# Two levels of an HGRN2 intra-chunk product as small matmuls at column positions of the TensorE array

## The chip, the core and the metric

The kernel runs on one core of a Trainium2 chip (trn2). A core has a matrix engine (TensorE, PE in the profile, with its weight loads shown apart as PEld), a vector engine (DVE), a scalar engine (ACT), GpSimd (POOL), a queue for transfers (SP) and 16 DMA engines. Matrix products are written to PSUM, and everything else lives in SBUF, both with 128 partitions. A matmul here has two operands: the stationary one, which a weight load (LDWEIGHTS) puts into the array, and the moving one, which streams through it.

The metric is the device time of one execution in microseconds (us). Before the change it is **1333.13 us**, the median of three runs (1332.87, 1333.13 and 1337.91).

## The reference

One layer of a decoder trunk on 512 tokens of width 1024: a wide projection feeds an mLSTM branch and an HGRN2 branch, the two are gated and merged, then a normalisation, a SwiGLU feed-forward block and a second normalisation. The change touches the HGRN2 branch alone, whose recurrence the reference writes in chunks:

```python
def step(state, xs):
    qc, kc, vc, lfc = xs
    a = jnp.cumsum(lfc, axis=2)
    rel = jnp.where(causal, a[:, :, :, None, :] - a[:, :, None, :, :], -jnp.inf)
    scores = jnp.einsum('bhtk,bhtsk,bhsk->bhts', qc, jnp.exp(rel), kc)
    o = (jnp.einsum('bhts,bhsv->bhtv', scores, vc)
         + jnp.einsum('bhtk,bhkv->bhtv', qc * jnp.exp(a), state))
    ...
```

For each of 8 heads (key size 128, value size 128), token t receives from every earlier token s the value of s, weighted by a product over the 128 key channels in which the forget gates between s and t enter channel by channel.

## The kernel before, in words

Everything is in 32-bit floats. The large projections split each operand into a high and a low part (`split`, lines 88 and 89: ACT writes the high part, DVE the low one) and add three products of the parts (`mm3`, lines 84 to 86). Each projection of 128 columns is 24 such matmuls with 512 moving columns, or, in `natural_proj`, many with 256 moving columns. Weights arrive through `load_w` and are split into three rotating buffers each, `whi` and `wlo` (lines 98 and 99).

The HGRN2 branch works on pairs of heads, `pr` = 0 to 3. `h_units` computes the forget gate f, the key K, the query Q, the value v and the output gate of a pair by projections. Then `h_chain` cuts the weights between tokens into levels. At a level with half-size `hs`, the tokens are cut into blocks of 2·hs, and the product of the K of each first half with the Q of the second half gives the weights across the middle of that block. After each level `h_advance` (lines 592 and 593) multiplies Q of the second halves and K of the first halves by the gates of their neighbours, so that the next level can use them; both are DVE operations of 128x512. The levels are hs = 1, 2 (by vector products), then 4, 8, 16, 32, 64, 128 and 256 by `h_level`.

In `h_level`, the levels 4, 8, 16 and 32 share one form: for each of the two heads (c) and each of the four tiles of 128 tokens (j), one matmul at line 646 has all 128 tokens of K as its stationary operand and the 64 tokens of Q that lie in second halves as its moving one. Its result is 128x64 in the PSUM tile `lps`, and for hs = 16 and 32 only hs·hs blocks of it are copied out, by ACT at line 673, to `ad`, the matrix of weights inside a tile. The level 64 (line 651) multiplies 64 stationary by 64 moving tokens, and 128 and 256 (lines 657 and 663) larger ones. A 32-bit matmul that is not split is two weight loads and two multiplies in the trace, called passes below, so the eight matmuls of a level are 16 passes.

The steps of a pair's chain are not run at once. `defer(t, ...)` puts each off by t units of work, and `tick`, called between projections, releases them. So the levels of one pair run between the projections of the next pair (for the last pair, between the merge gates), and the tile framework's scheduler, which orders each engine's instructions by its own estimate of when their operands are there, settles the exact place. Engines wait for each other by semaphores; PE takes its instructions in that order.

Of the kernel before, what the change touches and what calls it, by code (L numbers as in the profile page):

```python
# [15 lines left out]
P = 128  # L16
T = 512
NT = T // P
# [18 lines left out]
def tile_hybrid_trunk(  # L37
# [22 lines left out]
    nc = tc.nc  # L60
    xd, od, win = x[0], out[0], w_in[0]

    def pool(stack, name, bufs=1, space=None, side=None):
        kw = {}
        if space is not None:
            kw["space"] = space
        if side is not None:
            kw["side"] = side
        return stack.enter_context(tc.tile_pool(name=name, bufs=bufs, **kw))
# [39 lines left out]
    def psum(pl, tag, shape=(P, 512), bufs=None):  # L109
        kw = {} if bufs is None else {"bufs": bufs}  # L110
        return pl.tile(list(shape), F32, tag=tag, name=tag, **kw)
# [60 lines left out]
    px = pool(st_m, "px", bufs=2, space=PSUM)  # L172
# [334 lines left out]
    px = pool(st_px, "px2", bufs=5, space=PSUM)  # L507
# [80 lines left out]
    def h_advance(st, hs):  # L588
        nb = T // hs
        qv, kv = h_halves(st, hs)  # L590
        tv = st["cur"].rearrange("p (b two) -> p b two", two=2)
        nc.vector.tensor_mul(qv[:, :, 1, :], qv[:, :, 1, :], tv[:, :, 0:1].to_broadcast([P, nb, hs]))
        nc.vector.tensor_mul(kv[:, :, 0, :], kv[:, :, 0, :], tv[:, :, 1:2].to_broadcast([P, nb, hs]))
        if hs < 128:
            nt_ = st["tot"][:, st["toff"]:st["toff"] + nb]
            nc.vector.tensor_mul(nt_, tv[:, :, 0], tv[:, :, 1])
            st["cur"] = nt_
            st["toff"] += nb

    def h_place(st, ps, gs_, w, key):  # L600

        dst = st["ad"].rearrange("p j (g k) -> p j g k", k=gs_)[:, :, :, gs_ - w:]
        msk = masks[key].bitcast(U32)[:, None].to_broadcast([P, 8, P // gs_, w])
        nc.vector.copy_predicated(dst, msk, ps.rearrange("p j (g k) -> p j g k", k=w))
# [32 lines left out]
    def h_level(st, hs):  # L637

        K, Q, ad = st["K"], st["Q"], st["ad"]
        if hs < 64:  # L640
            lps = psum(px, "px", (P, 8, 64))
            for c in range(2):
                for j in range(NT):
                    js = slice(j * P, (j + 1) * P)
                    mov = Q[:, c, js].rearrange("p (g two h) -> p g two h", two=2, h=hs)[:, :, 1]
                    nc.tensor.matmul(lps[:, 4 * c + j], K[:, c, js], mov, start=True, stop=True)  # L646
        elif hs == 64:
            lps = psum(px, "px", (P, 8, 64))
            for c in range(2):
                for j in range(NT):  # L650
                    nc.tensor.matmul(lps[0:64, 4 * c + j], K[:, c, j * P:j * P + 64], Q[:, c, j * P + 64:(j + 1) * P],
                                     start=True, stop=True)
        elif hs == 128:
            lps = psum(px, "px", (P, 2, 2, P))
            for c in range(2):
                for b in range(2):
                    nc.tensor.matmul(lps[:, c, b], K[:, c, 2 * b * P:(2 * b + 1) * P],
                                     Q[:, c, (2 * b + 1) * P:(2 * b + 2) * P], start=True, stop=True)
        else:
            for c in range(2):  # L660
                lps = psum(px, "px", (P, 2, 256))
                for b in range(2):
                    nc.tensor.matmul(lps[:, b], K[:, c, b * P:(b + 1) * P], Q[:, c, 256:512],  # L663
                                     start=True, stop=True)
                nc.scalar.copy(st["a2"][:, c], lps)
            return
        h_advance(st, hs)
        if hs < 16:
            h_place(st, lps, 2 * hs, hs, hs)
        elif hs < 64:  # L670
            for g in range(64 // hs):
                rows_ = slice(2 * hs * g, 2 * hs * g + hs)
                nc.scalar.copy(ad[rows_, :, 2 * hs * g + hs:2 * hs * (g + 1)], lps[rows_, :, hs * g:hs * (g + 1)])
        elif hs == 64:
            nc.scalar.copy(ad[0:64, :, 64:128], lps[0:64])
        else:
            nc.scalar.copy(st["a1"], lps)
# [33 lines left out]
    def h_chain(st):  # L711

        steps = [(0, h_direct_0), (1, h_direct_1), (2, h_direct_2), (3, h_direct_3)]
        steps += [(t, lambda st, hs=hs: h_level(st, hs)) for t, hs in
                  ((3.5, 4), (4, 8), (4.5, 16), (5, 32), (5.5, 64), (6, 128), (6.5, 256))]
        steps += [(7 + 0.5 * c, lambda st, c=c: h_out(st, c)) for c in range(2)]
        for t, step in steps:
            if t:
                defer(t, lambda step=step: step(st))
            else:  # L720
                step(st)
# [194 lines left out]
```

## Time and profile before

| what | value |
|---|---|
| median of three runs | 1333.13 us |
| the profiled execution | 1334.2 us |
| its span, first to last instruction | 1332.5 us |
| TensorE clock granted, mean | 0.997 |
| DMA | 141.31 MB, mean 106 GB/s |

The page of the profile gives busy times per engine, then a row of digits over 40 slices of the span, then a chain of work traced back from the last instruction, then groups of instructions. In a row of a group, `128*64` is the shape of the stationary operand (partitions by columns), and `128x64` that of the moving one; `x256 | 30.5, 272` are the count, the busy time in us and the mean duration in ns of one. Durations of matmuls overlap, since the array is pipelined: the time that a run of them takes is read from the starts. A row of the timeline begins with the start and the duration in us; consecutive instructions of one kind are merged into one row with their count.

### The profile page before, as it was taken

What the parts mean: (1) busy time and instruction counts of PE and PEld (TensorE: products, weight loads), DVE (VectorE), ACT (ScalarE), POOL (GpSimd) and SP (SyncE); (2) the same over time, 40 slices, a digit from 0 to 9 for tenths busy, and PEclk for the clock granted to TensorE, in tenths of its full rate; (3) what the DMA queues carried; (4) which work ended last, traced back from release to release, by engine and by line L of the source; (5) the groups of instructions that cost most, each with busy time, mean ns of one, the idle gap of its engine ahead of it and who ended that gap; (6) DMA issues with size and microseconds to landing.
All of it is one profiled execution on the core that took longest, in us unless ns stands there. A gap on an engine that the chain in (4) does not pass through costs nothing.

```text
span 1332.5 us, 17405 instructions
## 1 busy us (share of the span) xinstructions
PE 1315.9 (99%) x7023; PEld 1136.1 (85%) x7023; DVE 753.9 (57%) x1140; ACT 537.0 (40%) x811; POOL 41.2 (3%) x78
## 2 busy tenths in 40 slices
PE   8999999999999999999999999999999999999997
PEld 7788889888988998889898988887898888888885
DVE  5764656566555755557586754345765433334575
ACT  4773553444342533332424333323773222233332
POOL 0000000000000002000000000000000000000001
PEclk9999999999999999999999999999999999999999
DMA  8222333233323323332232222235664343335672
GB/s 235 80 72 79 88 88 92 75 81 94 88 79 89 86 79 84 98 96 70 63 83 64 71 72 64 79 95 201 197 186 128 95 129 101 102 95 162 192 229 81
DMA packets 189424, 141.31 MB, mean 106 GB/s; under 512 B 5728, under 2 KB 178592, under 8 KB 189344
## 3 DMA queue, kind: packets, MB, share of 16 engines
q1 hardware_dynamic: 188288, 140.17, 37.0%
q8 instruction: 55, 0.90, 0.3%
q14 instruction: 25, 0.20, 0.0%
q10 hardware_dynamic: 1056, 0.03, 0.0%
HBM read 138.09 MB, written 2.10 MB: 105 GB/s over the span
## 4 chain that ended last, share of the span: by engine, by line
PE 97%; DVE 1%; ACT 1%; DMA 1%; issue 0%; POOL 0%; SPq 0%; DVEq 0%; POOLq 0%
PE pp L84 19%; PE pp L85 19%; PE pp L86 19%; PE pf L84 10%; PE pf L85 10%; PE pf L86 10%; PE px L646 2%; PE px L692 1%; PE s L85 1%; PE s L86 1%; PE s L84 1%; PE px L579 1%; DMA xn<-in_x_dram 1%; PE px L424 1%; PE px L663 1%; PE px L84 0%
## 5 line engine op out<-in xcount | busy, mean ns | idle before, releaser
L89 ACT CAST whi<-wraw 128x1024 fp32r<-128x1024 f32 x246 | 258.1, 1050 | 592.3 <-PE pp L85 253.8
L89 DVE TENSOR_TENSOR wlo<-wraw,whi 128x1024 fp32r<-128x1024 f32 x246 | 300.6, 1223 | 272.4 <-ACT whi L89 270.0
L84 PE MATMUL pp<-xh,whi 128*128 128x512 f32 x704 | 278.1, 395 | 0.0
L86 PE MATMUL pp<-xh,wlo 128*128 128x512 f32 x704 | 275.5, 391 | 0.0
L85 PE MATMUL pp<-xl,whi 128*128 128x512 f32 x704 | 275.4, 391 | 0.0
L86 PEld LDWEIGHTS pp<-xh,wlo 128*128 128x128 f32 x704 | 132.6, 188 | 28.3 <-issue 0.4
L84 PEld LDWEIGHTS pp<-xh,whi 128*128 128x128 f32 x704 | 132.7, 188 | 27.6 <-issue 1.0
L85 PEld LDWEIGHTS pp<-xl,whi 128*128 128x128 f32 x704 | 132.6, 188 | 26.2
L86 PE MATMUL pf<-x1h,wlo 128*128 128x512 f32 (+1 forms) x416 | 148.4, 357 | 0.8 <-DVE wlo L89 0.8
L84 PE MATMUL pf<-x1h,whi 128*128 128x512 f32 (+1 forms) x416 | 148.4, 357 | 0.0
L85 PE MATMUL pf<-x1l,whi 128*128 128x512 f32 (+1 forms) x416 | 148.3, 356 | 0.0
L84 PE MATMUL pp<-whi,xh 128*128 128x256 f32 x352 | 100.6, 286 | 0.0
L85 PE MATMUL pp<-wlo,xh 128*128 128x256 f32 x352 | 99.8, 284 | 0.0
L86 PE MATMUL pp<-whi,xl 128*128 128x256 f32 x352 | 99.5, 283 | 0.0
L86 PEld LDWEIGHTS pf<-x1h,wlo 128*128 128x128 f32 x416 | 78.6, 189 | 12.1 <-DVE wlo L89 1.0
L84 PEld LDWEIGHTS pf<-x1h,whi 128*128 128x128 f32 x416 | 78.6, 189 | 11.3
L85 PEld LDWEIGHTS pf<-x1l,whi 128*128 128x128 f32 x416 | 78.6, 189 | 11.3
L357 DVE SCALAR_TENSOR_TENSOR y<-u,cols,y 128x512 f32<-128x512 f32 x96 | 71.9, 750 | 6.1 <-ACT y L355 2.6
L85 PE MATMUL pf<-wlo,g 128*128 128x512 f32 x176 | 68.6, 390 | 0.0
L86 PE MATMUL pf<-whi,g 128*128 128x512 f32 x176 | 68.5, 389 | 0.0
L84 PE MATMUL pf<-whi,g 128*128 128x512 f32 x176 | 68.4, 389 | 0.0
L85 PEld LDWEIGHTS pp<-wlo,xh 128*128 128x128 f32 x352 | 67.5, 192 | 0.1
(251 smaller groups left out, 1940.3 us busy)
## 6 DMA issues: line engine op xcount, KB each, us to landing
wraw<-in_w_in_dram SPq DMA_DIRECT2D x110, 512.0 KB, 3.9
wraw<-in_w_ffn_down_dram SPq DMA_DIRECT2D x44, 512.0 KB, 3.6
wraw<-in_w_ffn_gate_dram SPq DMA_DIRECT2D x26, 512.0 KB, 3.9
wraw<-in_w_ffn_up_dram SPq DMA_DIRECT2D x26, 512.0 KB, 3.9
wraw<-in_w_proj_a_dram SPq DMA_DIRECT2D x16, 512.0 KB, 3.5
wraw<-in_w_out_dram SPq DMA_DIRECT2D x16, 512.0 KB, 3.8
wraw<-in_w_proj_b_dram SPq DMA_DIRECT2D x8, 512.0 KB, 4.3
xn<-in_x_dram SPq DMA_DIRECT2D x4, 512.0 KB, 5.0
```

The source lines that it names most:

```text
L84: nc.tensor.matmul(ps, lh, rh, start=start, stop=False, **kw)
L85: nc.tensor.matmul(ps, lh, rl, start=False, stop=False, **kw)
L86: nc.tensor.matmul(ps, ll, rh, start=False, stop=stop, **kw)
L89: return nc.scalar.copy(hi, src), nc.vector.tensor_sub(lo, src, hi.bitcast(F32))
L357: nc.vector.scalar_tensor_tensor(y, u[:, tap:tap + T], cwcol(tap, ch), y, op0=OP.mult, op1=OP.add)
L424: nc.tensor.transpose(tps[:, i * P:(i + 1) * P], hn[:, i, c * P:(c + 1) * P], ident)
L579: nc.tensor.matmul(ps.rearrange("p j n -> p (j n)"), ones_r, part.rearrange("p a b -> p (a b)"), start=(i == 0), stop=(i == 1))
L646: nc.tensor.matmul(lps[:, 4 * c + j], K[:, c, js], mov, start=True, stop=True)
L663: nc.tensor.matmul(lps[:, b], K[:, c, b * P:(b + 1) * P], Q[:, c, 256:512], start=True, stop=True)
L692: nc.tensor.matmul(ops[:, i], at, vc(j), start=(e == 0), stop=(e == len(terms) - 1))
```

## The change

`h_level` gets a branch of its own for hs = 16 and 32. In place of one matmul for a tile of 128 tokens there is one for each block: the K of its first half (hs tokens) is the stationary operand, the Q of its second half (hs tokens) the moving one. `tile_position=(0, s0)` puts the stationary operand at the columns s0 of the array, so that the result lands on the partitions s0 to s0 + hs of `lps`, where line 673 reads it. For hs = 16 the columns are 0, 32, 64 and 96; for hs = 32 they are 0 and 64. In the built program these matmuls are marked with an array tile of 128x32, those at line 651 with one of 128x64, and all projections with 128x128. Levels 4 and 8 keep the old form, now at line 656. The parts of `lps` that are no longer written were never read.

```diff
-        if hs < 64:
+        if hs in (16, 32):
+
+            lps = psum(px, "px", (P, 8, 64))
+            for c in range(2):
+                for j in range(NT):
+                    for g in range(64 // hs):
+                        s0 = 2 * hs * g
+                        nc.tensor.matmul(lps[s0:s0 + hs, 4 * c + j, hs * g:hs * (g + 1)],
+                                         K[:, c, j * P + s0:j * P + s0 + hs], Q[:, c, j * P + s0 + hs:j * P + s0 + 2 * hs],
+                                         start=True, stop=True, tile_position=(0, s0))
+        elif hs < 64:
             lps = psum(px, "px", (P, 8, 64))
```

For hs = 16 that is 8·4 = 32 matmuls in place of 8, and for hs = 32 it is 8·2 = 16, for each of four pairs. All lines below move down by ten.

The scheduler also moves a few neighbours. On PE, around the level hs = 32 of the first pair, the order before is (`px<-Q,K` is the level's product into PSUM; `pp<-...` are matmuls of a value projection):

```order
L86 MATMUL pp<-whi,xl 128x256
L84 MATMUL pp<-whi,xh 128x256
L646 MATMUL px<-Q,K 128x64 x8
L85 MATMUL pp<-wlo,xh 128x256
L86 MATMUL pp<-whi,xl 128x256
```

and after the change:

```order
L84 MATMUL pp<-whi,xh 128x256
L85 MATMUL pp<-wlo,xh 128x256
L647 MATMUL px<-Q,K 32x32 x16
L86 MATMUL pp<-whi,xl 128x256
L84 MATMUL pp<-whi,xh 128x256
```

The level stands one projection matmul later: 14 of them lie between the levels 16 and 32 where 13 did. This is so in the first three pairs; in the fourth, whose neighbours are 128x512 matmuls, 7 lie between them where 12 did.

On DVE, at the same place, one piece of the difference (`e<-K,Q` is the first product of the next pair, `v<-pp,vb` the value with its bias, `Q<-Q,tot` and `K<-K,tot` the advance after a level):

```order
 L89 TENSOR_TENSOR wlo<-wraw,whi 128x1024
-L571 TENSOR_TENSOR e<-K,Q 128x512
 L592 TENSOR_TENSOR Q<-Q,tot 128x16x32
 L593 TENSOR_TENSOR K<-K,tot 128x16x32
 L556 TENSOR_TENSOR v<-pp,vb 128x512
+L571 TENSOR_TENSOR e<-K,Q 128x512
 L592 TENSOR_TENSOR Q<-Q,f 128x512
 L593 TENSOR_TENSOR K<-K,f 128x512
-L571 TENSOR_TENSOR e<-K,Q 128x512
 L556 TENSOR_TENSOR v<-pp,vb 128x512
+L571 TENSOR_TENSOR e<-K,Q 128x512
```

The two products of the next pair moved behind the advance of level 32 and the values.

On DVE in the fourth pair (`wlo<-wraw,whi` is the low part of a projection's weights, `acc<-acc,sga` a merge gate that is applied; line 730 became 740):

```order
 L604 COPY_PREDICATED ad_4702<-mask_4696,px 128x64x8
-L89 TENSOR_TENSOR wlo<-wraw,whi 128x1024
 L592 TENSOR_TENSOR Q<-Q,tot 128x32x16
 L593 TENSOR_TENSOR K<-K,tot 128x32x16
-L730 TENSOR_TENSOR acc<-acc,sga 128x512
+L740 TENSOR_TENSOR acc<-acc,sga 128x512
+L89 TENSOR_TENSOR wlo<-wraw,whi 128x1024
 L592 TENSOR_TENSOR Q<-Q,tot 128x16x32
 L593 TENSOR_TENSOR K<-K,tot 128x16x32
```

The split of a weight's low part moved behind the advance of level 16 and the gate. The rows of ACT, POOL and SP stand in the same order as before.

## The prediction

> **What bounds the kernel now.** I read the page first, for the busy shares and the chain that ended last.
>
> ```profile
> PE 1315.9 (99%) x7023; PEld 1136.1 (85%) x7023; DVE 753.9 (57%) x1140; ACT 537.0 (40%) x811; POOL 41.2 (3%) x78
> ...
> PE 97%; DVE 1%; ACT 1%; DMA 1%; issue 0%; POOL 0%; SPq 0%; DVEq 0%; POOLq 0%
> ```
>
> TensorE is busy for 99% of the span and makes up 97% of the chain. The levels of the HGRN2 chain lie between 600 and 830 us. The table by windows gives busy times in the order PE, PEld, DVE, ACT, POOL, then the clock:
>
> ```profile
> 600.00:830.00 230.00, 230.00 (x1419) 204.20 (x1418) 151.27 (x221) 81.49 (x173) 6.30 (x7) 1.00 0.27 70
> ```
>
> PE has no idle time there, at full clock. DVE is busy for two thirds of it and ACT for a third, so neither sets the pace. What the change gives or costs is therefore what it does to PE's own time in this stretch. Busy PE is not PE at its peak, so I read the time of a level from starts in the timeline. Level 16 of the first pair, between projection matmuls of 256 columns:
>
> ```profile
> 617.95 0.28 PE L86 MATMUL pp<-whi,xl 128*128 128x256 f32 x1
> 617.95 1.88 PEld L646 LDWEIGHTS px<-Q,K 128*128 128x128 f32 x16
> 618.07 1.90 PE L646 MATMUL px<-Q,K 128*128 128x64 f32 x16
> ...
> 619.78 0.36 PE L84 MATMUL pp<-whi,xh 128*128 128x256 f32 x1
> ...
> 619.98 0.28 PE L85 MATMUL pp<-wlo,xh 128*128 128x256 f32 x1
> ```
>
> From the start of L86 to that of L85 are 2.03 us. L86 and L84 take 0.12 us each of these (617.95 to 618.07 is one such step), so the level costs **1.79 us**. Its 16 weight loads follow each other every (1.88 - 0.19)/15 = 0.113 us, and 16 times that is 1.8: the level is nothing but its loads of 128 columns, and its 64 moving columns are hidden behind them. The first load starts together with the projection's last multiply, so there is no gap on entry.
>
> Level 32 of the same pair, with the advance of level 16 ahead of it on DVE:
>
> ```profile
> 620.01 0.69 DVE L592 TENSOR_TENSOR Q<-Q,tot 128x512 f32<-128x512 f32 x1 [0.67 <-PE px L646]
> ...
> 620.62 0.69 DVE L593 TENSOR_TENSOR K<-K,tot 128x512 f32<-128x512 f32 x1
> ...
> 621.28 0.28 PE L84 MATMUL pp<-whi,xh 128*128 128x256 f32 x1
> 621.42 1.86 PEld L646 LDWEIGHTS px<-Q,K 128*128 128x128 f32 x16
> 621.45 1.97 PE L646 MATMUL px<-Q,K 128*128 128x64 f32 x16
> ...
> 623.23 0.36 PE L85 MATMUL pp<-wlo,xh 128*128 128x256 f32 x1
> ...
> 623.43 0.28 PE L86 MATMUL pp<-whi,xl 128*128 128x256 f32 x1
> ```
>
> Counted in the same way it is 623.43 - 621.28 - 0.24 = **1.91 us**, 0.12 more: K's advance ends at 621.31, and the first load starts behind it at 621.42, not with the multiply at 621.28. In the fourth pair the neighbours have 512 columns:
>
> ```profile
> 811.16 0.39 PE L84 MATMUL pp<-xh,whi 128*128 128x512 f32 x1
> ...
> 811.38 0.39 PE L85 MATMUL pp<-xl,whi 128*128 128x512 f32 x1
> ...
> 811.61 1.89 PE L646 MATMUL px<-Q,K 128*128 128x64 f32 x16
> ...
> 813.63 0.39 PE L84 MATMUL pp<-xh,whi 128*128 128x512 f32 x1
> ...
> 813.86 0.40 PE L85 MATMUL pp<-xl,whi 128*128 128x512 f32 x1
> ```
>
> Here 813.63 - 811.38 = 2.25, less two steps of 0.23, is 1.79: no wait. Before, the two levels take 4 x 1.79 (level 16) + 3 x 1.91 + 1.79 (level 32) = **14.68 us** of PE. No more than that, 1.1% of the time, is at stake.
>
> **The change, part by part.** It removes these 14.68 us and adds, per pair, 64 passes for level 16 and 32 for level 32, each a load and a multiply, in array tiles of 128x32. The nearest row that stands in a narrower array tile is level 64 (128x64):
>
> ```profile
> 627.26 0.28 PE L85 MATMUL pp<-wlo,xh 128*128 128x256 f32 x1
> ...
> 627.38 0.28 PE L86 MATMUL pp<-whi,xl 128*128 128x256 f32 x1
> 627.59 1.01 PEld L651 LDWEIGHTS px<-Q,K 128*64 128x64 f32 x16
> 627.59 1.15 PE L651 MATMUL px<-Q,K 128*64 128x64 f32 x16
> ...
> 628.67 0.50 PE L84 MATMUL pp<-xh,whi 128*128 128x512 f32 x1
> ...
> 629.00 0.39 PE L85 MATMUL pp<-xl,whi 128*128 128x512 f32 x1
> ...
> 629.23 0.39 PE L86 MATMUL pp<-xh,wlo 128*128 128x512 f32 x1
> ```
>
> Two things are read here. First, loads of 64 columns come every (1.01 - 0.14)/15 = 0.058 us, against 0.113 for 128: a straight line, 0.86 ns a column and 3 ns on top. Second, the level costs 629.00 - 627.38 - 0.12 - 0.23 = 1.27 us where 16 x 0.058 is 0.93. The other **0.34 us** lie at its two ends: the first load waits until 0.21 us after the start of the multiply ahead, not 0.00 as in level 16, and behind the level L84 to L85 takes 0.33, not 0.23. I put that down to the change of the array's tile size, since no other engine is named as the cause, and charge it to each of the eight new levels, 2.72 us. Its other bound is nothing, if a narrow load needs no such pause.
>
> [...]
>
> For the step of one pass I have two bounds. By the line above, a load of 16 columns takes 0.017 us and one of 32 columns 0.031. The upper bound is the shortest step that a run of plain 32-bit load and multiply pairs shows, 0.058, should that be the step of the pair and not of the load. Between them stand rows with small operands:
>
> ```profile
> 52.26 0.34 PEld L304 LDWEIGHTS px<-ident,gs 128*4 128x4 f32 x4
> 52.29 0.60 PE L304 MATMUL px<-ident,gs 128*4 128x128 f32 x4
> ...
> 52.62 0.19 PEld L84 LDWEIGHTS pp<-xh,whi 128*128 128x128 f32 x1
> ...
> 52.65 0.48 PE L84 MATMUL pp<-xh,whi 128*128 128x512 f32 x1
> ```
>
> The shortest distance from a load to its multiply is 0.03 us, even for a load of 4 columns, and the next load can start with that multiply (617.95, both). I take 0.031 us a pass for level 16, nearest to these rows, and 0.032 for level 32, where line and floor agree. So I expect the passes one behind the other, with no gain from standing side by side:
>
> - level 16: 64 x 0.031 + 0.34 = 2.32 us, against 1.79: +0.53, four times: +2.12;
> - level 32: 32 x 0.032 + 0.34 = 1.36 us, against 1.91 three times and 1.79 once: -1.65 and -0.43.
>
> The sum is **+0.04 us**, nothing. At 0.017 and 0.031 it is -3.65; without the 0.34 at the ends, another -2.7, so -6.4. At 0.058 for both, level 16 costs 4.05 and level 32 2.20: +9.04, +0.87 and +0.41 make +10.3.
>
> [...]
>
> What is moved costs nothing. The advance of level 16 needs 620.01 to 621.31, and the first load came 621.42 - 619.78 = 1.64 us after the first projection matmul behind the level. Now 14 steps of 0.12 and the pause on leaving give 1.7 to 1.9 us of cover (fourth pair: 7 of 0.23, 1.6, with the pause 1.8), so the wait of 0.12 goes; should the cover fail, it comes back, at most 0.5 us in all. The split `wlo` that DVE does later in the fourth pair is delayed by some 2 us; it fills one of three buffers, while the two others hold 24 matmuls of 0.23 each, 5.5 us apiece. In the list of PE's waits over the whole run (total, times, longest) such a split stands once, for 0.8 us at another tile (`pf`):
>
> ```profile
> PE pf L84 <- DVE sgb L741: 0.9, 1, 0.9
> PE pf L86 <- DVE wlo L89: 0.8, 1, 0.8
> ```
>
> The products `e` that moved behind the values are wanted a pair's projections later. ACT's copies have the same number and size.
>
> **The rivals.**
>
> *Each change of column position drains the array (slower).* Successive matmuls stand at different columns: 32 changes in level 16 and 16 in level 32, 48 x 4 = 192. Entering level 64 cost 0.21 - 0.12 = 0.09 us of waiting and some 0.05 more for a load that nothing hides (0.058 less the 3 ns of handing over). At 0.14 each the changes cost 26.9 us: 1360 us. It would make a slower kernel from 0.035 us a change on (192 x 0.035 = 6.7 us). For it: no row before has two positions in one level. [...]
>
> *A pair has a floor of its own at 0.058 (slower).* The sum is then +10.3: 1343.4 us; it passes 6.7 us from 0.049 a pass. For it: nothing shorter is seen in a run of plain pairs. Against it: the step of 0.113 is twice that for twice the columns, with 3 ns on top, so 0.058 looks like the load of 64 columns and not like a floor.
>
> *The positions work side by side (faster).* If the four passes of a group in level 16, and the two in level 32, took the time of one, the levels would cost 16 x 0.031 + 0.34 and 16 x 0.032 + 0.34, 1.69 us a pair, 6.76 in place of 14.68: -7.9, 1325.2 us. Against it: loads are never closer than 0.058 in these rows, and loads, not multiplies, were what the levels consisted of. [...]
>
> **How the numbers follow.** The profiled execution took 1334.2 us, 1.1 above the median of 1333.13; the change of +0.04 is put on the median, 1333.2 us. A measurement of this kernel tells 0.5%, 6.7 us, from no change. Forecast with its lower bounds (-6.4 to +6.7): 0.72. Floor near 0.058: 0.10. Drain at each position: 0.13. Side by side: 0.05. Slower is the second and third, 0.23. The range reaches from the lower bound, 1327, to the floor's 1343.4, rounded to 1344; the drain and the side-by-side case are left out, 0.18.
>
> **What would show it.** Steps of 0.03 between loads at line 647; 2.3 us for level 16 and 1.4 for level 32, counted as above; a first load some 0.2 us behind the multiply ahead; level 32's first load no longer behind K's advance. Steps of 0.05 and more between every second load, or loads nearly on top of each other, would prove me wrong in the one way or the other; so would a PE that waits for DVE between 600 and 830 us.

## The result, and the profile after

The changed kernel takes **1324.82 us** (median of four runs, 1324.70 to 1328.28). The kernel before takes 1334.72 in the four runs now at hand (1332.87 to 1337.91). The ratio is **0.993**, with a 95% interval of 0.9911 to 0.9949: faster by 0.5 to 0.9%. The forecast was 1333.2 us with a range of 1327 to 1344, and the time lies below it.

The page after, first the busy shares and then the chain:

```profile
span 1322.9 us, 17916 instructions
...
PE 1306.4 (99%) x7279; PEld 1124.9 (85%) x7279; DVE 752.2 (57%) x1140; ACT 536.4 (41%) x811; POOL 41.1 (3%) x78
...
PE 94%; DVE 2%; ACT 2%; issue 1%; DMA 1%; POOL 0%; SPq 0%; DVEq 0%; POOLq 0%; ACTq 0%
```

PE is still busy for 99% of a span that is 9.6 us shorter, with 256 passes more (7279 against 7023). Nothing else took over. Where the 9.6 us went is read from starts: that of level 4 of the first pair and that of level 256 of the last pair, in the timeline of PE alone. First the kernel before, then the changed one (the counts in these rows end with the window that was read):

```profile
608.75 0.44 PE L646 MATMUL px<-Q,K 128*128 128x64 f32 x3
...
824.08 1.24 PE L663 MATMUL px<-Q,K 128*128 128x256 f32 x5
```

```profile
607.37 0.33 PE L656 MATMUL px<-Q,K 128*128 128x64 f32 x2
...
814.59 0.38 PE L673 MATMUL px<-Q,K 128*128 128x256 f32 x1
```

This **stretch of levels** went from 215.33 to 207.23 us, **8.10 less**. The other 1.4 us lie ahead of it (608.75 to 607.37), in code that the change does not touch: by the traces they are there already after the first 15 us. Behind the stretch the two kernels agree within 0.1. What lies ahead varies from one execution to the next. The table by windows (busy times of PE, PEld, DVE, ACT and POOL, then the clock, the DMA share and the rate) shows it at 60 to 80 us, first in the changed kernel and then in a second profile of the same kernel, in which the levels start at 612.44:

```profile
60.00:80.00 20.00, 20.00 (x90) 15.53 (x89) 9.59 (x13) 18.83 (x32) 5.56 (x16) 1.00 0.24 61
```

```profile
60.00:80.00 20.00, 19.96 (x71) 14.52 (x72) 6.30 (x9) 16.55 (x29) 5.57 (x16) 0.83 0.10 27
```

The mean granted clock over these 20 us is 0.83 in the second profile, since for 6.8 us of them it is 0.50, and 71 multiplies are counted in place of 90. Of the 5.07 us between the two starts of the levels, 1.9 are there already at 50 us, by the traces; the 3.2 that are added between 50 and 87 us are near the 3.4 that 6.8 us at half of the clock make. The runs of one kernel spread over 4 to 5 us, so the experiments below are compared by level and by the stretch, not by their totals.

Level 16 of the first pair after the change, from the timeline of PE and then that of its loads:

```profile
616.56 0.28 PE L86 MATMUL pp<-whi,xl 128*128 128x256 f32 x1
616.77 0.70 PE L647 MATMUL px<-Q,K 128*16 128x16 f32 x64
617.40 0.39 PE L84 MATMUL pp<-whi,xh 128*128 128x256 f32 x1
617.62 0.28 PE L85 MATMUL pp<-wlo,xh 128*128 128x256 f32 x1
```

```profile
616.77 0.59 PEld L647 LDWEIGHTS px<-Q,K 128*16 128x16 f32 x64
```

Counted as in the prediction, 617.62 - 616.56 - 0.24 = **0.82 us**, where 2.32 were forecast and 1.79 stood before. The 64 loads take 0.59 us together, about 0.008 from one to the next: a quarter of the 0.031 that I had allowed each. The pause ahead of the level is as forecast, 0.21 us from L86 to the first pass.

Level 32 with the advance ahead of it, in the same two views and DVE's:

```profile
618.47 0.68 DVE L593 TENSOR_TENSOR K<-K,tot 128x512 f32<-128x512 f32 x1
...
619.05 0.28 PE L85 MATMUL pp<-wlo,xh 128*128 128x256 f32 x1
...
619.27 0.62 PEld L647 LDWEIGHTS px<-Q,K 128*32 128x32 f32 x32
619.30 0.70 PE L647 MATMUL px<-Q,K 128*32 128x32 f32 x32
...
619.93 0.39 PE L86 MATMUL pp<-whi,xl 128*128 128x256 f32 x1
...
620.15 0.28 PE L84 MATMUL pp<-whi,xh 128*128 128x256 f32 x1
```

It takes 620.15 - 619.05 - 0.24 = **0.86 us** (1.36 forecast, 1.91 before). Its loads are (0.62 - 0.11)/31 = 0.016 us apart, half of 0.032, with 0.11 the length of one. K's advance ends at 619.15, and the first load comes at 619.27, 0.22 behind L85, where 0.21 is the pause alone. So of the wait of 0.12 at most 0.04 is left (0.86, where 0.82 is what the level takes without a wait, in an experiment below). In the fourth pair the two levels take 0.82 and 0.83. Together that is 4 x 0.82 + 3 x 0.86 + 0.83 = 6.7 us in place of 14.7, which are the 8 us.

### The profile page after: what moved, and what is told of

Same layout as the page of the kernel before. It is cut to its first block, busy times and chain, and to the rows that moved or that the text cites. A ratio compares the mean times of both kernels' runs of the same rounds, so it can differ in the third digit from the quotient of the medians.

```text
span 1322.9 us, 17916 instructions
## 1 busy us (share of the span) xinstructions
PE 1306.4 (99%) x7279; PEld 1124.9 (85%) x7279; DVE 752.2 (57%) x1140; ACT 536.4 (41%) x811; POOL 41.1 (3%) x78
## 4 chain that ended last, share of the span: by engine, by line
PE 94%; DVE 2%; ACT 2%; issue 1%; DMA 1%; POOL 0%; SPq 0%; DVEq 0%; POOLq 0%; ACTq 0%
PE pp L84 19%; PE pp L86 19%; PE pp L85 19%; PE pf L86 9%; PE pf L84 9%; PE pf L85 9%; PE px L702 1%; PE s L85 1%; PE s L86 1%; PE px L656 1%; PE s L84 1%; PE px L579 1%; ACT xt L825 1%; DMA xn<-in_x_dram 1%; PE px L424 1%
## 5 line engine op out<-in xcount | busy, mean ns | idle before, releaser
L86 PE MATMUL pp<-xh,wlo 128*128 128x512 f32 x704 | 275.7, 392 | 0.0
L85 PE MATMUL pp<-xl,whi 128*128 128x512 f32 x704 | 275.2, 391 | 0.0
L86 PEld LDWEIGHTS pp<-xh,wlo 128*128 128x128 f32 x704 | 132.6, 188 | 28.2 <-issue 0.4
L85 PEld LDWEIGHTS pp<-xl,whi 128*128 128x128 f32 x704 | 132.6, 188 | 26.4
L86 PE MATMUL pf<-x1h,wlo 128*128 128x512 f32 (+1 forms) x416 | 148.4, 357 | 0.7 <-DVE wlo L89 0.7
L85 PE MATMUL pf<-x1l,whi 128*128 128x512 f32 (+1 forms) x416 | 148.3, 356 | 0.0
L86 PE MATMUL pp<-whi,xl 128*128 128x256 f32 x352 | 99.8, 284 | 0.0
L85 PE MATMUL pp<-wlo,xh 128*128 128x256 f32 x352 | 99.6, 283 | 0.0
L86 PEld LDWEIGHTS pf<-x1h,wlo 128*128 128x128 f32 x416 | 78.6, 189 | 12.2 <-DVE wlo L89 0.9
L85 PEld LDWEIGHTS pf<-x1l,whi 128*128 128x128 f32 x416 | 78.6, 189 | 11.3
L85 PE MATMUL pf<-wlo,g 128*128 128x512 f32 x176 | 68.6, 390 | 0.0
L86 PE MATMUL pf<-whi,g 128*128 128x512 f32 x176 | 68.5, 389 | 0.0
L84 PEld LDWEIGHTS pp<-whi,xh 128*128 128x128 f32 x352 | 67.4, 192 | 0.2
```

The lines of the kernel that those rows point to most:

```text
L84: nc.tensor.matmul(ps, lh, rh, start=start, stop=False, **kw)
L85: nc.tensor.matmul(ps, lh, rl, start=False, stop=False, **kw)
L86: nc.tensor.matmul(ps, ll, rh, start=False, stop=stop, **kw)
```

## The experiments

Theory A: products at different column positions of the array run side by side; at one position a pass needs its own time. Rival B: a narrow array tile makes loads cheap wherever they stand. Rival C, on order: the array finds free positions by itself in its queue. All times of levels are those of the first pair, counted in one way. The kernels of the experiments down to the change of tile size by itself were executed once each; in every one of them level 16 takes the same time in all four pairs to 0.01 us. In all these kernels a product at column position p is also written to the partitions of PSUM from p on, so no run here tells these two apart: "position" stands for both.

**All at one position.** `at` replaces the column position, and the copies read from there:

```diff
-  nc.tensor.matmul(lps[s0:s0 + hs, ...], ..., tile_position=(0, s0))
+  at = 0
+  nc.tensor.matmul(lps[at:at + hs, ...], ..., tile_position=(0, at))
-  nc.scalar.copy(ad[rows_, ...], lps[rows_, ...])
+  nc.scalar.copy(ad[rows_, ...], lps[at:at + hs, ...])
```

> Theory A (positions run side by side): with every small product at column position 0 the passes can only follow each other, at the 0.025 us (16 columns, four times the 0.0064 seen in the changed kernel) and 0.032 us (32 columns) that one position allows. Level 16: 64 x 0.025 + 0.31 = 1.9 us, level 32: 32 x 0.032 + 0.31 = 1.3 us, against 0.82 and 0.86; the span about 6 us longer than the changed kernel's. Theory B (a narrow array tile makes every load cheap, wherever it stands): both levels stay at 0.82 and 0.86.

Level 16 in the timeline of PE, and its loads:

```profile
618.17 0.28 PE L86 MATMUL pp<-whi,xl 128*128 128x256 f32 x1
618.38 1.76 PE L648 MATMUL px<-Q,K 128*16 128x16 f32 x64
620.08 0.39 PE L84 MATMUL pp<-whi,xh 128*128 128x256 f32 x1
620.30 0.28 PE L85 MATMUL pp<-wlo,xh 128*128 128x256 f32 x1
```

```profile
618.38 1.66 PEld L648 LDWEIGHTS px<-Q,K 128*16 128x16 f32 x64
```

Level 16 takes 1.89 us and level 32 1.32, the stretch 213.53: 6.30 us more than the change. The same products in the same narrow tiles cost 1.89 us in place of 0.82 and 1.32 in place of 0.86 when they share a position. B falls. The loads are (1.66 - 0.09)/63 = 0.025 us apart; those of level 32 are 0.032 apart.

**Two positions for level 16.** As above, with `at = s0 % 64 if hs == 16 else s0`.

> Level 16 at two positions (0 and 32) in place of four, level 32 unchanged. Theory A: half of 0.025 a pass, 64 x 0.0125 + 0.31 = 1.1 us for level 16, 0.86 for level 32. Theory B: 0.82 and 0.86.

```profile
621.50 0.28 PE L86 MATMUL pp<-whi,xl 128*128 128x256 f32 x1
621.71 0.97 PE L648 MATMUL px<-Q,K 128*16 128x16 f32 x64
622.62 0.39 PE L84 MATMUL pp<-whi,xh 128*128 128x256 f32 x1
622.84 0.28 PE L85 MATMUL pp<-wlo,xh 128*128 128x256 f32 x1
```

Level 16 takes 622.84 - 621.50 - 0.24 = 1.10 us, as A expected; level 32, unchanged, 0.82. One, two and four positions give 1.89, 1.10 and 0.82. Less 0.3 at the ends that is 1.6, 0.8 and 0.5: the time halves with two, and with four it falls by a factor of three. By the trace, the steps between the loads of level 16 are in turn 0.007 and 0.018 us with two positions, 0.025 together, which is the step that one position has alone. The same holds for 32 columns, in the changed kernel: 0.002 and 0.030, together the 0.032 of one position. So with two positions each kept its own step, and the passes of the other fell between.

**One position after the other.** The loop over positions goes outermost:

```diff
-  for c in range(2):
-      for j in range(NT):
-          for g in range(64 // hs):
+  for g in range(64 // hs):
+      for c in range(2):
+          for j in range(NT):
```

> Four positions as in the change, but all products of one position first, then those of the next. Theory A with passes taken in order: neighbours share a position, so nothing runs side by side and the levels cost what one position costs, 1.9 and 1.3 us. Theory C (the array takes loads for a free position out of its queue ahead of others): most of the gain stays, near 0.9 us. Theory B: 0.82 and 0.86.

```profile
618.25 0.28 PE L86 MATMUL pp<-whi,xl 128*128 128x256 f32 x1
618.46 1.52 PE L647 MATMUL px<-Q,K 128*16 128x16 f32 x64
619.91 0.39 PE L84 MATMUL pp<-whi,xh 128*128 128x256 f32 x1
620.13 0.28 PE L85 MATMUL pp<-wlo,xh 128*128 128x256 f32 x1
```

Level 16 takes 1.64 us and level 32 1.22, between one position (1.89 and 1.32) and the change (0.82 and 0.86), much nearer to the first. The stretch is 212.05. For the gain, neighbours in the order had to stand at different positions. C holds for a few passes only: around each of the three changes of position in level 16 three multiplies start 0.005 to 0.006 us behind the one ahead and the four next to them 0.019 to 0.020; after the first few passes, all others are 0.025 apart.

**The first head's products three times.** `for c in (0, 0, 0, 1)` in place of `range(2)`; the repeated products write the same values again.

> The first head's products are issued three times, the second's once: 128 passes in level 16, 64 in level 32. Theory A: the cost at the ends (0.31) stays and passes cost 0.0064 to 0.0085 us each, so level 16 is 1.2 to 1.4 us and level 32 is 64 x 0.016 + 0.31 = 1.3. If the slower rhythm of the second half of level 16 is a queue that has run empty after 32 passes, the rhythm changes after 32 passes again (1.33 us in all); if it belongs to the second head's operands, it changes after 96 (1.2 us).

The loads of level 16 as a whole, and those that start in the first 0.24 us, from windows of the timeline:

```profile
620.41 1.12 PEld L647 LDWEIGHTS px<-Q,K 128*16 128x16 f32 x128
```

```profile
620.41 0.31 PEld L647 LDWEIGHTS px<-Q,K 128*16 128x16 f32 x34
```

Level 16 takes 1.35 us, so 64 passes more cost 0.53 and the ends stay. Of the loads, 34 start in 0.24 us, 0.007 apart; the other 94 start in the next 0.79 (1.12 - 0.09 - 0.24), 0.0084 apart. The rhythm changes after some 32 passes, as in the changed kernel, and not with the head, and the 1.35 us are near the 1.33 expected for that case. Whether a queue is behind it, no run shows. Level 32 came to 1.71 us where 1.3 was expected, since DVE's advance of K ended late (it held the first multiply back by 0.31 us by the trace): a miss of mine, since I had not counted how much of PE's work covers the advance in this kernel.

**One level at a time.** `if hs == 16:` in the one kernel and `if hs == 32:` in the other.

> Level 16 alone in the new form, level 32 as before. If the two parts add up: level 16 at 0.82 us, level 32 at 1.79 to 1.91, so about 3.9 us of the 8.0 that the chain of levels lost in the changed kernel. If they help or hinder each other, the level that is as before shows it (a wait for the advance on DVE, above 1.91).

> Level 32 alone in the new form: level 16 at 1.79, level 32 at 0.83 to 0.97 (the wait of up to 0.12 for K's advance may stay), about 4.1 us less in the chain of levels.

With level 16 alone it takes 0.82 and the old level 32 1.99 in the first three pairs; the stretch is 211.68, 3.65 less than before. With level 32 alone it takes 0.82 and the old level 16 1.79; the stretch is 211.09, 4.24 less. The parts, 7.89, add up to the 8.10 but for 0.2. A shorter level 16 lengthens the wait for K's advance, from 0.12 to 0.20. The new level 32 hides the wait even in its old place: with level 32 alone 13 projection matmuls lie between the two levels, as before, K's advance ends 0.02 us after the start of the multiply ahead (621.48 and 621.46 by the trace), and the first load, which comes 0.21 after that start at the change of tile size, does not have to wait for it.

**The change of tile size by itself.** The kernel before, with a block written once more in a narrow tile:

```diff
                 nc.tensor.matmul(lps[:, 4 * c + j], K[:, c, js], mov, start=True, stop=True)
+        if hs in (16, 32):
+            nc.tensor.matmul(lps[0:16, 0, 0:16], K[:, 0, 0:16], Q[:, 0, hs:hs + 16], start=True, stop=True,
+                             tile_position=(0, 0))
```

> The kernel before, with one matmul of 16x16 in a 128x32 array tile behind the eight of levels 16 and 32 (it writes a block once more). If the 0.31 us at the ends of a level are the price of changing the array's tile size, each of the eight levels is longer by 0.31 and two passes, 0.33 to 0.36 us, 2.6 to 2.9 us in all. If they belong to the first and last operands of a level (or to a wait on another engine), it is the two passes alone, 0.05 us each, 0.4 us in all.

```profile
621.79 0.28 PE L86 MATMUL pp<-whi,xl 128*128 128x256 f32 x1
621.91 1.90 PE L646 MATMUL px<-Q,K 128*128 128x64 f32 x16
623.74 0.22 PE L648 MATMUL px<-Q,K 128*16 128x16 f32 x2
623.88 0.38 PE L84 MATMUL pp<-whi,xh 128*128 128x256 f32 x1
624.10 0.28 PE L85 MATMUL pp<-wlo,xh 128*128 128x256 f32 x1
```

Level 16 takes 624.10 - 621.79 - 0.24 = 2.07 us, 0.28 more than before: less than the 0.33 expected, but far from the 0.05 that two passes alone would cost. In level 32 it is 0.16 in the first three pairs, where the wait of 0.12 is absorbed, and 0.28 in the fourth. The stretch is 217.24, 1.91 more than before, between the two expectations (2.6 to 2.9 and 0.4) and nearer to the first. So a visit of two passes already cost 0.28 us in level 16, most of the 0.3 that lie at the ends of a new level.

**More levels in the new form.** If A is right, levels 4 and 8 gain from it as well, with 32 stationary by 16 moving tokens at four positions, and so does level 64 with every second product at column 64:

```diff
-  nc.tensor.matmul(lps[:, 4 * c + j], K[:, c, js], mov, start=True, stop=True)
+  for s0 in range(0, P, 32):
+      js = slice(j * P + s0, j * P + s0 + 32)
+      mov = Q[:, c, js].rearrange("p (g two h) -> p g two h", two=2, h=hs)[:, :, 1]
+      nc.tensor.matmul(lps[s0:s0 + 32, 4 * c + j, s0 // 2:s0 // 2 + 16], K[:, c, js], mov,
+                       start=True, stop=True, tile_position=(0, s0))
...
-  nc.tensor.matmul(lps[0:64, 4 * c + j], K[...], Q[...], start=True, stop=True)
+  nc.tensor.matmul(lps[64 * (j % 2):64 * (j % 2) + 64, 4 * c + j], K[...], Q[...],
+                   start=True, stop=True, tile_position=(0, 64 * (j % 2)))
```

The copies follow: four masked ones of 32 partitions on DVE for a level of 4 or 8, two on ACT for level 64.

> On top of the change, levels 4 and 8 are cut into four products of 32 stationary by 16 moving tokens, at the columns 0, 32, 64 and 96. Theory A: a pass of 32 columns needs 0.032 us at one position, a quarter of that with four side by side, but no less than the 0.0085 of a run of more than 32 passes: 64 passes in 0.53 us, and 0.31 at the ends, 0.84 per level against 1.79. Eight levels: 7.6 us less than the changed kernel, 1317 us, a ratio of 0.987 to 0.988 to the kernel before. Rival: DVE, which now places the blocks by four small operations in place of one (0.70 us), or its advance holds the next level back, and up to half of the gain comes back as waits of PE between levels.

> On top of the change, level 64 puts every second product at column 64. Theory A: two positions of 64 columns side by side halve the step of 0.058, 16 x 0.029 + 0.34 = 0.80 us against 1.27, four times 0.46, 1.9 us less than the changed kernel, 1323 us. If only tiles of 32 columns run side by side, level 64 stays at 1.27.

> Both of these. Theory A: the gains add, 9.5 us less than the changed kernel, 1315 us, a ratio of 0.986 to the kernel before. If waits for DVE take the place of PE's work, the sum is less than the parts.

> The changed kernel once more, beside the three kernels with more levels in the new form and on the same chip: 8.0 us less than the kernel before in the levels, a ratio of 0.994, should the rest of the 0.993 first measured be the start of the run, which no part of the change touches.

Measured side by side, against seven runs of the kernel before (median 1336.28):

| kernel | median, us | ratio, 95% interval | stretch of levels, us |
|---|---|---|---|
| the change again | 1327.93 | 0.9938 (0.9917 to 0.9959) | 207.23 |
| and levels 4, 8 | 1320.21 | 0.9883 (0.9865 to 0.9900) | 201.16 |
| and level 64 | 1323.80 | 0.9905 (0.9887 to 0.9924) | 205.43 |
| and levels 4, 8, 64 | **1319.01** | **0.9871** (0.9855 to 0.9887) | 199.26 |

The change repeats its 8.1 us in the stretch to 0.01. Levels 4 and 8 give 6.07 of the 7.6 expected: each takes 0.86 in place of 1.79, but level 32 rises from 0.86 to 1.30 in three pairs. The timeline of the kernel with all three, DVE and PE, shows why:

```profile
616.57 0.69 DVE L571 TENSOR_TENSOR e<-K,Q 128x512 f32<-128x512 f32 x1
617.29 1.23 DVE L609 TENSOR_TENSOR Q<-Q,f 128x1024 f32<-128x1024 f32 x1
618.43 0.68 DVE L592 TENSOR_TENSOR Q<-Q,tot 128x512 f32<-128x512 f32 x1
619.03 0.69 DVE L593 TENSOR_TENSOR K<-K,tot 128x512 f32<-128x512 f32 x1
```

```profile
619.87 0.70 PE L647 MATMUL px<-Q,K 128*32 128x32 f32 x32 [0.41 <-DVE K L593]
```

When level 16 ends (the next projection matmul starts at 616.93 by the trace), DVE is at the product `e` of line 571 and then takes that of line 609, so the advance starts 1.5 us behind the level, where it was 0.47 in the changed kernel, and PE waits for it. That is the rival named for this run, at a fifth of the gain where up to a half was allowed. The four copies of level 8 take 1.28 us on DVE by the trace, where the one took 0.71; besides, a split of weights and the product `e` stand ahead of the advance here and did not in the changed kernel. How much of the wait each of these makes is not shown. Level 64, in its own kernel:

```profile
625.50 0.28 PE L86 MATMUL pp<-whi,xl 128*128 128x256 f32 x1
625.70 0.69 PE L661 MATMUL px<-Q,K 128*64 128x64 f32 x16
626.32 0.50 PE L84 MATMUL pp<-xh,whi 128*128 128x512 f32 x1
626.65 0.39 PE L85 MATMUL pp<-xl,whi 128*128 128x512 f32 x1
```

626.65 - 625.50 - 0.12 - 0.23 = 0.80, as expected, where 1.27 stood. By the trace its loads are in turn 0.006 to 0.007 and about 0.05 us apart, together the 0.058 of one position: two tiles of 64 columns run side by side too. The two gains add up (199.26 = 207.23 - 6.07 - 1.80, less 0.1), to 8.0 us where 9.5 were expected. The kernel with all of it has the shortest stretch; its total does not stand clear of that with levels 4 and 8, since the intervals of the two ratios overlap.

## Why the prediction was wrong, point by point

- *PE alone counts in this stretch, and at most 14.68 us are at stake.* Right: PE is busy for 230.00 of the 230 us from 600 on, before and after, and the whole gain lies in those levels.
- *The ends of a narrow level cost 0.34 us.* Right in kind, a little large in size: 1.89 - 64 x 0.025 = 0.29 with one position, 0.30 for level 32, and 0.28 for a visit of two passes with those included. What the array does in that time, no run shows. Eight levels make it 0.3 to 0.4 us too much in the sum.
- *A pass takes 0.031 us at 16 columns and 0.032 at 32.* At one position it is 0.025 and 0.032. The first, taken from the distance of a load to its multiply, was 0.006 too long, 1.5 us in the sum. That distance was misread: 0.03 us is not the shortest, since in the prediction's own rows of level 64 the first load and the first multiply both start at 627.59. With these two sizes mended, the forecast for products at one position would have been -1.8 us, and the kernel with one position has just that (215.33 to 213.53).
- *"The passes one behind the other, with no gain from standing side by side."* **This is the step that failed**, and it is worth 6.30 us, from 213.53 to 207.23. I held that loads are served one at a time because no two stood closer than 0.058 us before. But every run of loads in that trace stood at one position, so the row could not speak about two. The rival "the positions work side by side", priced at -7.9 us and given 0.05, is what happened: -8.1. That its price came so near is partly luck: it took four passes of level 16 at 0.031 us, where four take about 0.025 in the first half of the level and 0.034 in the second.
- *Drain at each position; a floor of 0.058 for a pair.* Neither is there: 0.006 to 0.0085 us between passes at four positions, and 0.025 at one.
- *What is moved costs nothing.* Right but for 0.04 us: the wait of level 32 for K's advance was to go, and it shrank from 0.12 to 0.04, because DVE was still at the product of line 609 when level 16 ended and began the advance 0.47 us behind it (617.87 by the trace, 617.40 the next projection matmul), not 0.23 as before. PE has no other wait between 600 and 830 us. (In the fourth pair 11 projection matmuls lay between the two levels before the change, by the trace, not 12.)

## What to carry to other kernels

In these kernels the same small products cost PE less the more column positions take turns: 1.89, 1.10 and 0.82 us for 64 passes at one, two and four positions. So give small products whose results may land on different partitions different positions, and let the inner loop alternate between them. Each visit to another tile size cost 0.28 to 0.34 us here, which a level must earn back: eight matmuls of 128 columns were enough here (1.79 to 0.82). And a row that shows a resource used in one way only, here one position, gives no bound on its use in another; a rival that no row contradicts deserves more than 0.05.

## What the runs showed of the hardware that was not expected

- Passes of 16 columns start 0.006 to 0.007 us apart over four positions for the first 32, then 0.0085 on average, whichever head's operands they have; at one position they are 0.025 apart from the third pass on.
- With two positions in turn, each kept the step that it has alone: 0.025 us for 16 columns, 0.032 for 32, and 0.058 for 64, where the whole level went from 1.27 to 0.80 us with two positions.
- When the position changes only after 16 passes, a few passes of the next position still started early (0.005 to 0.006 us behind the one ahead), and the level gained 0.25 us of the 1.07 that alternating gives.
- Between 60 and 80 us the mean granted clock is 0.83 in one profile of the changed kernel, 0.50 for 6.8 us of them, and 1.00 in the other; that goes with some 3.2 of the 5.07 us between their starts of the levels.
